# Values first, q and k of the forgetting attention and four dilated tiles as seven-product blocks, all through DRAM

## The chip, the core and the metric

One core of one Trainium2 chip runs the whole kernel in one launch. The metric is the device time of one execution in microseconds, lower is better, given as the median of several runs. TensorE multiplies matrices (PE in the views; PEld is its weight load), VectorE (DVE), ScalarE (ACT) and GpSimd (POOL) do elementwise work, and SyncE (SP) mostly starts transfers. Each engine works through its own queue in a fixed order, and waits at its head for what the next instruction needs.

## The reference

One decoder layer on x of 1024 tokens by 1024 channels, in float32:

```python
h = rms_norm(x, norm_mix_g)
proj = h @ w_in            # q, k, v of 3 dilated groups (256 wide each), then q, k, v of FoX (512 wide each), 8 forget logits, 2 x 1024 gates
...                        # dilated attention of each group; the groups are joined by their softmax denominators
...                        # FoX: softmax(q.k / 8 + sum of log f between key and query), 8 heads of 64, causal
gates = sigmoid(proj[..., o4:] + b_gate)
x = x + (gate0 * (dil @ w_dil_out) + gate1 * (fox @ w_fox_out)) @ w_out
...                        # then a SwiGLU feed-forward of width 2816 and a last norm
```

FoX is the forgetting attention: the logits get the cumulated log of a forget gate, c[t] - c[s].

## The kernel before

Every large product splits each operand in a high part (type fp32r) and a low part, the rest (`split`, L94 to L96: the high part by ScalarE, the low part by VectorE) and multiplying three times (`mm3`, L98 to L101): high by high, high by low, low by high. `projT` (L183) does the same for a transposed result with its lines L189, L190 and L193. One tile of 128 output channels for all 1024 tokens is therefore 2 halves x 8 slices of the depth x 3 = 48 products of 512 columns. A scheduler places all instructions ahead of the run: each engine gets one fixed order. Two sorts of PSUM banks exist: `pd` (the main program) and `pf` (filler).

The stages, in the order of the program:

- **x tiles and FoX values** (L271 to L316). For each of eight tiles of 128 tokens: norm, transpose into hT (L166, L171, split at L95/L96), then `values` of the tile before (L296): two groups of 24 products, 256 and 264 columns wide, where the last 8 columns are the forget logits (L307). The values stay in SBUF (`vf`).
- **Running sums** (L317 to L352, `cums`): log of the forget gate from the logits, in nine small operations on VectorE and ScalarE (L328 to L338), a product with a triangle and one with ones (L342, L343), and `negc` (L345 to L350).
- **FoX attention** (L354 to L468): four pairs of heads. `fox_proj` makes q and k of a pair (two tiles of 48 products), then come scores, maximum, exponentials, values and denominators for two halves of the queries. Scores of a unit stand ahead of the values of the unit before.
- **Dilated attention** (L474 to L650): tables for the distance bias, `dilv` (the values of the three groups, L509 to L521), then for two pairs of heads (u) and two halves of the queries (b) scores (L262), exponentials, values (L632), denominators (L635), `finish` (L243 to L253) and the store of the output (L638).
- **Merge** (L658 to L700): `load_o` reads the attention outputs back (L669) and splits them into `oh` and `ol`; `merge` multiplies each with its output weights (`projT`, L189 first), and with the gate.
- The output projection, then the feed-forward with its seven-product blocks (`up`, L853, 84 products instead of 96 for two tiles, from four combinations of its input and from three combinations of its weights made on GpSimd, L844 to L849), and the last norm.

Filler: `ahead` (L213) makes one tile of 48 products into the banks `pf`, evacuates it on ScalarE (L223) and stores it to DRAM (L224). There are 28: the 12 q and k tiles of the dilated attention (`dil_ahead`), and the 16 gate tiles (`gates_ahead`). They have their own weight buffers. The scheduler places their products wherever the main program's would wait; they run beside FoX, the dilated values, the dilated attention and the merge.

Of the kernel before, what the change touches and what calls it, by code (L numbers as in the profile page):

```python
# [15 lines left out]
P = 128  # L16
# [31 lines left out]
def layer_kernel(  # L48
# [152 lines left out]


    g_dram = dpool.tile([2 * KT, P, S], F32, name="g_dram")
    qk_dram = dpool.tile([2, 3, 2, P, S], F32, name="qk_dram")
    STR = ((1, 4, 8), (1, 8, 8))
    f_ctx = pool_of("ahead", 1, side="right")
    fpool = f_ctx.__enter__()
# [5 lines left out]
    def ahead(c0, dst, dl=1, sc=1.0):  # L213
        pf = [psf.tile([P, HALF], F32, tag="f", name=nm("pf")) for _ in range(2)]
        for c in range(2):
            w = load_w(w_in[c * HALF:(c + 1) * HALF, c0:c0 + P], 4, P, tag="fw", pool=fpool, rpool=fpool)
            for hh in range(2):
                for k in range(4):
                    mm3(pf[hh][:], w[:, k], hT[hh][:, 4 * c + k], c == 0 and k == 0, c == 1 and k == 3)
        n = HALF // dl  # L220
        st = fpool.tile([P, dl, S // dl], F32, tag="fst", name=nm("fst"), bufs=2)
# [4 lines left out]
    def dil_ahead():  # L226
        for u in range(2):
            for g in range(3):
                for a in range(2):
                    ahead(a * DIL_W + g * 256 + u * P, qk_dram[u, g, a], STR[a][g], SCALE if a == 0 else 1.0)  # L230

    def gates_ahead():
        for br, dt in merge_order:
            ahead(GATE0 + (br * KT + dt) * P, g_dram[br * KT + dt])
# [36 lines left out]
    with pool_of("fox", 1) as spool:  # L271
        lf = spool.tile([P, NT, 8], F32, name="lf", bufs=1)

        with pool_of("foxv", 2) as vpool:
            xts, last_x = [], [None]

            def load_x():
                i = len(xts)
                if i < NT:
                    xts.append(vpool.tile([P, D], F32, tag="xt", name=nm("xt"), bufs=4))  # L280
                    last_x[0] = nc.sync.dma_start(out=xts[i][:], in_=x[i * P:(i + 1) * P, :])

            load_x()
            gain1 = load_gain(vpool, norm_mix_g)
            nc.gpsimd.memset(ones[:], 1.0)
            vf = spool.tile([P, NT, 4, 2, DH], F32, name="vf", bufs=1)
            bg = cpool.tile([P, 16], F32, name="bg")
            bf = cpool.tile([P, 8], F32, name="bf")
            nc.gpsimd.dma_start(out=bf[0:1, :], in_=b_fgt[0:1, :])
            with nc.allow_non_contiguous_dma("per-partition gate bias"):  # L290
                nc.gpsimd.dma_start(out=bg[:], in_=b_gate[0].rearrange("(k p) -> p k", p=P))
            nc.gpsimd.partition_broadcast(bf[:], bf[0:1, :])
            wv = load_w(w_in[:, FOX0 + 2 * FOX_W:GATE0], KT, FOX_W + 8, tag="wv", bufs=1, pool=vpool,
                        chunk=P, rpool=vpool, rbufs=3, shared=2 * P, between=load_x)

            def values(i):  # L296
                hh, c = divmod(i * P, HALF)
                for c0, n in ((0, 256), (256, 264)):
                    pv = pd()
                    for k in range(KT):  # L300
                        mm3(pv[:, :n], hT[hh][:, k, c:c + P], wv[:, k, c0:c0 + n], k == 0, k == KT - 1)
                    p0 = c0 // 128
                    nc.vector.tensor_copy(
                        vf[:, i, p0:p0 + 2],
                        pv[:, :256].rearrange("p (a b d) -> p a b d", a=2, b=2))
                    if n == 264:
                        nc.vector.tensor_tensor(out=lf[:, i, :], in0=pv[:, 256:264], in1=bf[:],  # L307
# [661 lines left out]
```

## Time and profile before

| what | before |
|---|---|
| median of 3 runs | 1524.32 us (1521.35 to 1524.67) |
| profiled execution | 1523.66 us |
| its span, first to last instruction | 1522.0 us |
| PE / PEld busy | 1486.5 / 1213.7 us |
| DVE / ACT / POOL busy | 841.7 / 526.0 / 355.9 us |
| mean granted TensorE clock | 0.994 |
| moved by DMA | 148.56 MB |

The profiled execution is one run of the same program under the hardware profiler; the 1.7 us between it and its span lie before its first and after its last instruction. A row of a group reads: line, engine, operation, tile written <- tiles read, size, count, then busy time and mean ns of one, then the idle time of that engine just before and what ended it. A matmul's row gives the time from its start to its end; since matmuls overlap in the pipeline, what one costs is the distance from its start to the next one's start. A row of the timeline starts with its start time and its length.

### The profile page before, as it was taken

The page shows a single profiled execution, that of the slowest core. Times are in us where ns is not written, and L with a number is a line of the kernel's source. Part 1 is how long each engine was busy: PE and PEld are TensorE (multiplying, and loading weights), DVE is VectorE, ACT ScalarE, POOL GpSimd, SP SyncE. Part 2 cuts the span into 40 slices and gives each one's busy share as a digit, 9 for nine tenths or more (in the row PEclk, how much of TensorE's full clock was granted, in tenths as well). Part 3 has the DMA queues.
Part 4 walks back from the last instruction along what each step waited for, and adds up shares of the span by engine and source line. Part 5 has one row for each costly group of instructions (what it writes and reads, how often), then busy time and mean ns, then how long its engine had stood idle before and what let it go on. Part 6 is the DMA issues. An engine that isn't in the chain of part 4 may idle for free.

```text
span 1522.0 us, 18443 instructions
## 1 busy us (share of the span) xinstructions
PE 1486.5 (98%) x7172; PEld 1213.7 (80%) x7172; DVE 841.7 (55%) x1329; ACT 526.0 (35%) x828; POOL 355.9 (23%) x303
## 2 busy tenths in 40 slices
PE   6999999999999999999999999999999999999997
PEld 6987777777997778888888778888888887888886
DVE  6439687683129983115628854444444445856546
ACT  5246566553003244224315422222222225312113
POOL 0012224231001110000000245555555552140000
PEclk9999999999999999999999999999999999999999
DMA  8012211134113226334613122222222225642202
GB/s 251 14 57 62 66 60 43 35 91 132 70 35 132 70 77 218 104 100 149 239 56 138 42 69 84 83 84 83 83 84 84 83 98 198 205 136 86 95 14 97
DMA packets 130471, 148.56 MB, mean 98 GB/s; under 512 B 6352, under 2 KB 104656, under 8 KB 130384
## 3 DMA queue, kind: packets, MB, share of 16 engines
q1 hardware_dynamic: 117712, 103.86, 22.4%
q10 hardware_dynamic: 6768, 22.55, 4.1%
q0 software_dynamic: 5904, 20.98, 3.7%
q8 instruction: 56, 0.92, 0.2%
q14 instruction: 31, 0.25, 0.0%
HBM read 109.62 MB, written 37.75 MB: 97 GB/s over the span
## 4 chain that ended last, share of the span: by engine, by line
PE 89%; DMA 3%; ACT 2%; DVE 2%; POOL 2%; issue 1%; SPq 1%; ACTq 0%; DVEq 0%
PE pd L774 20%; PE pd L99 10%; PE pd L100 10%; PE pd L101 10%; PE pf L99 7%; PE pf L100 7%; PE pf L101 7%; PE pd L189 4%; PE pd L193 4%; PE pd L190 4%; PE pd L448 2%; DMA wr<-in_w_ffn_in_dram 2%; ACT wh L95 1%; PE pd L262 1%; PE pd L397 1%; PE pd L398 1%
## 5 line engine op out<-in xcount | busy, mean ns | idle before, releaser
L95 ACT ACTIVATE wh<-wr 128x1024 fp32r<-128x1024 f32 (+2 forms) x187 | 154.7, 836 | 472.6 <-PE pf L100 153.9
L96 DVE TENSOR_TENSOR wl<-wr,wh 128x1024 fp32r<-128x1024 f32 (+2 forms) x187 | 181.1, 974 | 205.0 <-ACT wh L95 198.4
L774 PE MATMUL pd<-hT_t,wh 128*128 128x512 f32 x640 | 198.4, 391 | 2.4 <-ACT c L860 2.4
L99 PE MATMUL pf<-hT_t,wh 128*128 128x512 f32 x448 | 177.0, 395 | 0.0
L100 PE MATMUL pf<-hT_t,wh 128*128 128x512 f32 x448 | 176.7, 394 | 0.0
L101 PE MATMUL pf<-hT_t,wl 128*128 128x512 f32 x448 | 174.1, 394 | 0.0
L774 PE MATMUL pd<-tT,wh 128*128 128x512 f32 x480 | 148.2, 390 | 0.4 <-DVE v L778 0.4
L774 PEld LDWEIGHTS pd<-hT_t,wh 128*128 128x128 f32 x640 | 120.6, 189 | 27.6 <-ACT c L860 2.8
L99 PE MATMUL pd<-wh,wh 128*128 128x512 f32 x352 | 138.0, 393 | 3.6 <-DVE acc L920 2.3
L100 PE MATMUL pd<-wl,wh 128*128 128x512 f32 x352 | 137.6, 391 | 0.0
L101 PE MATMUL pd<-wh,wl 128*128 128x512 f32 x352 | 137.6, 391 | 0.0
L99 PE MATMUL pd<-wh,hT_t 128*128 128x512 f32 (+2 forms) x384 | 128.1, 343 | 5.2 <-ACT wh L95 3.5
L100 PE MATMUL pd<-wl,hT_t 128*128 128x512 f32 (+2 forms) x384 | 131.3, 343 | 0.8 <-DVE t L155 0.6
L101 PE MATMUL pd<-wh,hT_t 128*128 128x512 f32 (+2 forms) x384 | 131.0, 342 | 0.0
L774 PE MATMUL pd<-hT_t,wl 128*128 128x512 f32 x320 | 126.6, 396 | 0.6 <-DVE wl L96 0.2
L920 DVE TENSOR_TENSOR acc<-pd,acc 128x512 f32<-128x512 f32 x128 | 86.0, 686 | 70.7 <-PE pd L101 70.5
L844 POOL TENSOR_TENSOR s<-wr 128x512 f32<-128x512 f32 x20 | 34.5, 1723 | 332.2 <-DVE tT L96 264.4
L774 PEld LDWEIGHTS pd<-tT,wh 128*128 128x128 f32 x480 | 90.3, 188 | 19.6 <-DVE v L778 0.8
L99 PEld LDWEIGHTS pf<-hT_t,wh 128*128 128x128 f32 x448 | 84.9, 190 | 20.7 <-issue 2.5
L101 PEld LDWEIGHTS pf<-hT_t,wl 128*128 128x128 f32 x448 | 84.6, 189 | 20.5 <-issue 3.1
L100 PEld LDWEIGHTS pf<-hT_t,wh 128*128 128x128 f32 x448 | 84.8, 189 | 19.8 <-issue 2.8
L774 PE MATMUL pd<-tT,wl 128*128 128x512 f32 x240 | 93.2, 389 | 0.0
(198 smaller groups left out, 2647.4 us busy)
## 6 DMA issues: line engine op xcount, KB each, us to landing
wr<-in_w_ffn_in_dram SPq DMA_DIRECT2D x44, 512.0 KB, 4.0
wr<-in_w_in_dram SPq DMA_DIRECT2D x56, 256.0 KB, 3.0
wr<-a_dram SPq DMA_DIRECT2D x22, 512.0 KB, 4.2
wr<-in_w_ffn_down_dram SPq DMA_DIRECT2D x22, 512.0 KB, 3.7
a_dram<-a POOLq DMA_DIRECT2D x20, 512.0 KB, 5.0
wr<-in_w_in_dram SPq DMA_DIRECT2D x18, 512.0 KB, 4.4
g_dram<-fst ACTq DMA_DIRECT2D x16, 512.0 KB, 3.2
land<-g_dram SPq DMA_DIRECT2D x16, 512.0 KB, 3.4
```

The lines of the kernel that those rows point to most:

```text
L95: nc.scalar.activation(out=hi, in_=src, func=AF.Copy)
L96: nc.vector.tensor_tensor(out=lo, in0=src, in1=hi.bitcast(F32), op=ALU.subtract)
L99: nc.tensor.matmul(psum, w.hi, m.hi, start=start, stop=False)
L100: nc.tensor.matmul(psum, w.hi, m.lo, start=False, stop=False)
L101: last_mm[0] = nc.tensor.matmul(psum, w.lo, m.hi, start=False, stop=stop)
L189: nc.tensor.matmul(pt[hh][:], w.hi[:, k], m.hi, start=(k == 0), stop=False)
L190: nc.tensor.matmul(pt[hh][:], w.hi[:, k], m.lo, start=False, stop=False)
L193: nc.tensor.matmul(pt[hh][:], w.lo[:, k], m.hi, start=False, stop=(k == kt - 1))
L448: nc.tensor.matmul(po[half[e], HALF - width[j]:], vf[:, j, pr, e], L[:, off[j]:off[j + 1]], start=(j == nj - 1), stop=(j == 0), skip_group ...
L774: last_mm[0] = nc.tensor.matmul(bank[:], p, q, start=first and k == 0 and n == 0, stop=k == 3 and n == 2, skip_group_check=True)
L844: nc.gpsimd.tensor_tensor(out=s12[:, :4], in0=u1, in1=u2, op=ALU.add)
L920: nc.vector.tensor_tensor(out=acc[:, t, cs], in0=pt[:], in1=acc[:, t, cs], op=ALU.add)
```

## The change

1. **FoX values** leave the attention's pool: they are computed as before, but for tiles 2 to 7 as one group of 24 products 512 columns wide, without the forget logits, and each tile is stored to DRAM (`vf_dram`, on GpSimd's queue). The attention loads all of them in one transfer.
2. **Dilated values** (`dilv`) come right after, ahead of both attentions: first group 0 with the forget logits beside it (`w0`, 264 columns), then groups 1 and 2 together (`w12`, 512 columns). ScalarE evacuates them (VectorE did) and they go to `vd_dram`.
3. **Combinations.** Beside that, `form` makes four combinations T1 to T4 of the quarters of h (16 adds of 128x1024 on VectorE, and their splits). They stay in SBUF until the projections end.
4. **The running sums** come after the dilated values, with `lf` and `negc` now in a pool of their own.
5. **Projections.** Six blocks make two tiles each with seven half-products instead of eight (84 products of 512 columns): four for q and k of FoX, two for q and k of the dilated groups 0 and 1 of u = 0. The weights' combinations are made on GpSimd (`left_side`). Results go to DRAM (`fqk_dram`, `dqk_dram`). All of this has no filler.
6. **Attentions.** `fox_qk` loads q and k of a pair from DRAM instead of computing them, and splits them. The filler that remains is 24 tiles: 8 dilated q and k tiles (`BESIDE`) and the 16 gates. `ahead` loads its weights as one tile through the common weight buffers. The dilated attention loads its values from DRAM.
7. The feed-forward's helpers (`raw_w`, `pair_of`, `prod`, `left_side`) move up to be shared; its work is the same. From the output projection on, TensorE's order is the same.

The core of the diff:

```diff
-    def ahead(c0, dst, dl=1, sc=1.0):
+    def ahead(pool, c0, dst, dl=1, sc=1.0):
...
-        for c in range(2):
-            w = load_w(w_in[c * HALF:(c + 1) * HALF, c0:c0 + P], 4, P, tag="fw", pool=fpool, rpool=fpool)
...
+        w = load_w(w_in[:, c0:c0 + P], KT, P)
+        for hh in range(2):
+            for k in range(KT):
+                mm3(pf[hh][:], w[:, k], hT[hh][:, k], k == 0, k == KT - 1)
...
+    TWOS = [[(0, g, a) for g in range(2)] for a in range(2)]
+    BESIDE = [(0, 2, 0), (0, 2, 1)] + [(1, g, a) for g in range(3) for a in range(2)]
...
+    def left_side(pool, rg, ru, bufs):
+        g1, g2, u1, u2 = rg[:, :4], rg[:, 4:], ru[:, :4], ru[:, 4:]
+        A1 = pair_of(rg[:])
+        s12 = pool.tile([P, KT, P], F32, tag="s", name=nm("s12"), bufs=2)
+        nc.gpsimd.tensor_tensor(out=s12[:, :4], in0=u1, in1=u2, op=ALU.add)
+        nc.gpsimd.tensor_tensor(out=s12[:, 4:], in0=s12[:, :4], in1=g1, op=ALU.subtract)
+        S12 = pair_of(s12[:], KT, pool, "s12", bufs)
...
+    def projections(pool, T, c, dst, dls, sc):
+        T1, T2, T3, T4 = T
+        A1, S12, S34, A22 = left_side(pool, *[raw_w(w_in[:, c0:c0 + P]) for c0 in c], 1)
...
+        prod(b1, A1[:, :4], B11, True)
+        copy(flat[0], b1)
+        prod(b2, S12[:, 4:], T2, True)
+        join(flat[1], b2, cc)
+        prod(b1, A1[:, 4:], B21)
+        copy(o1[:, :, :n1], b1, dls[0])
+        prod(b2, S34[:, :4], T3)
+        join(flat[2], b2, cc)
+        prod(b3, S12[:, :4], T1, True)
+        join(o2[:, :, n2:], b3, v3, dls[1])
+        prod(b2, A22, T4)
+        join(o2[:, :, :n2], b2, cc, dls[1])
+        prod(b3, S34[:, 4:], B22)
+        join(o1[:, :, n1:], b3, v2, dls[0])
...
         def values(i):
+            n = 256 if i < 2 else FOX_W
+            for c0 in range(0, FOX_W, n):
...
+                nc.vector.tensor_copy(st[:, c0:c0 + n], pv[:, :n])
+            nc.gpsimd.dma_start(out=vf_dram[i], in_=st[:])
...
+        def form(k0):
...
+            back(f3, B11)
+            back(f2, B12)
+            back(f4, B22)
+            vec(f1, f2, f3)
+            keep(T1, f1)
+            vec(f2, f4, f2)
+            keep(T3, f2)
+            vec(f4, f4, f1)
+            keep(T2, f4)
+            back(f3, B21)
+            vec(f3, f3, f4)
+            keep(T4, f3)
...
+            for g0, w, n in ((0, w0, 264), (1, w12, 512)):
+                for tt in range(NT):
...
+                    nc.scalar.activation(out=st[:, :m], in_=pv[:, :m], func=AF.Copy)
...
+            form(0)
+            form(2)
...
+        with pool_of("proj", 1) as upool:
+            for pr in range(0, 4, 2):
+                for a in range(2):
+                    c0 = FOX0 + a * FOX_W + pr * P
+                    projections(upool, T, (c0, c0 + P), [fqk_dram[a, pr + i] for i in range(2)], (1, 1), 1.0)
+            for two in TWOS:
+                projections(upool, T, [dil_cols(*t) for t in two], [dqk_dram[t] for t in two],
+                            [STR[a][g] for u, g, a in two], (SCALE, 1.0)[two[0][2]])
...
-        def fox_proj(pool, ql, pr):
+        def fox_qk(pool, ql, pr):
...
+                    raw = pool.tile([P, S], F32, tag="qraw", name=nm("qraw"), bufs=2)
+                    for at in half:
+                        nc.sync.dma_start(out=raw[at, :], in_=fqk_dram[a, pr, half[e], :])
+                    nc.scalar.activation(out=xs[e][:], in_=raw[:], func=AF.Copy, scale=sc)
...
-    with tc.issue_after(last_x[0].ins):
-        dil_ahead()
+    for u, g, a in BESIDE:
+        ahead(fpool, dil_cols(u, g, a), dqk_dram[u, g, a], STR[a][g], (SCALE, 1.0)[a])
...
-    with tc.issue_after(last_x[0].ins):
-        gates_ahead()
+    for br, dt in merge_order:
+        n = br * KT + dt
+        ahead(fpool, GATE0 + n * P, g_dram[n])
```

How the instructions move is shown at three places.

First, VectorE at the end of the FoX values. Before, the copies of the last tiles (`vf`) and the logits (`lf`) are followed by the running sums (L328 on):

```order
84 L303 COPY vf<-pd_700 128x256
85 L303 COPY vf<-pd_726 128x256
86 L307 TENSOR_TENSOR lf<-pd_726,bf 128x8
87 L303 COPY vf<-pd_753 128x256
88 L303 COPY vf<-pd_779 128x256
89 L307 TENSOR_TENSOR lf<-pd_779,bf 128x8
90 L328 TENSOR_SCALAR t_816<-lf 128x64
91 L329 TENSOR_TENSOR az<-lf,t_816 128x64
```

In the changed kernel adds of the combinations (L400, tiles f) stand there, then the copy of the last FoX values (L378), and behind it the low parts of w0, the weights of the dilated values of group 0 (L96 wv, three chunks), ahead of the combinations' splits (tT):

```order
74 L400 TENSOR_TENSOR f_1148<-f_1150,f_1148 128x1024
75 L400 TENSOR_TENSOR f_1149<-hT_t 128x1024
76 L400 TENSOR_TENSOR f_1150<-f_1150,f_1147 128x1024
77 L400 TENSOR_TENSOR f_1149<-f_1149,f_1150 128x1024
78 L378 COPY vst_623<-pd_624 128x512
79 L96 TENSOR_TENSOR wv_662<-wr_663,wv_661 128x8x128
80 L96 TENSOR_TENSOR wv_662<-wr_667,wv_661 128x8x128
81 L96 TENSOR_TENSOR wv_662<-wr_671,wv_661 128x8x8
82 L96 TENSOR_TENSOR tT_655<-f_1147,tT_655 128x1024
```

The low parts of these weights now stand behind a copy that needs the last value product, and no filler stands in the order there.

Second, TensorE around the two products of the running sums (`lf` with `upper` and with `ones`). Before, filler of a gate or a dilated tile (pf) stands ahead of them and a product of q behind them:

```order
435 L100 MATMUL pf_2555<-hT_t,wh_2587 128x512
436 L101 MATMUL pf_2555<-hT_t,wl_2588 128x512
437 L99 MATMUL pf_2556<-hT_t,wh_2587 128x512
438 L342 MATMUL pd_828<-lf,upper 128x64
439 L343 MATMUL pd_828<-lf,ones 128x64
440 L189 MATMUL pd_859<-hT_t,wh_853 128x512
441 L190 MATMUL pd_859<-hT_t,wh_853 128x512
```

In the changed kernel the last products of the dilated values (`wv` with `hT_t`) stand ahead, and the first block of the projections (L272) behind:

```order
638 L99 MATMUL pd_1119<-wv_659,hT_t 128x512
639 L100 MATMUL pd_1119<-wv_660,hT_t 128x512
640 L101 MATMUL pd_1119<-wv_659,hT_t 128x512
641 L475 MATMUL pd_1208<-lf,upper 128x64
642 L476 MATMUL pd_1208<-lf,ones 128x64
643 L272 MATMUL pd_1251<-hT_t,wh_1229 128x512 x2
644 L272 MATMUL pd_1251<-hT_t,wl_1230 128x512
645 L272 MATMUL pd_1251<-hT_t,wh_1229 128x512 x2
```

The sums' products moved from the middle of filler to the seam between the dilated values and the projections.

Third, TensorE at the end of the dilated attention: the last products with values (vd), the denominators (Mx with ones), filler (pf), and the merge's first products (oh). Before, 63 filler products stand between the denominators and the merge:

```order
2680 L632 MATMUL pd_4408<-L_541_4236,vd 64x64
2681 L632 MATMUL pd_4408<-L_540_4235,vd 64x64
2682 L635 MATMUL pd_4409<-Mx_4242,ones 64x512
2683 L635 MATMUL pd_4409<-Mx_4241,ones 64x512
2684 L100 MATMUL pf_4916<-hT_t,wh_4948 128x512
2685 L101 MATMUL pf_4916<-hT_t,wl_4949 128x512
...
2746 L101 MATMUL pf_4983<-hT_t,wl_5015 128x512
2747 L189 MATMUL pd_5542<-oh_5514,wh_5536 128x512
2748 L189 MATMUL pd_5543<-oh_5514,wh_5536 128x512
```

In the changed kernel four do:

```order
2695 L761 MATMUL pd_4350<-L_602_4177,vd 64x64
2696 L764 MATMUL pd_4351<-Mx_4184,ones 64x512
2697 L764 MATMUL pd_4351<-Mx_4183,ones 64x512
2698 L101 MATMUL pf_5297<-hT_t,wl_5299 128x512
2699 L99 MATMUL pf_5297<-hT_t,wh_5298 128x512
2700 L100 MATMUL pf_5297<-hT_t,wh_5298 128x512
2701 L101 MATMUL pf_5297<-hT_t,wl_5299 128x512
2702 L189 MATMUL pd_5388<-oh_5360,wh_5382 128x512
2703 L189 MATMUL pd_5389<-oh_5360,wh_5382 128x512
```

All gate tiles are now made ahead of this point; before, 399 filler products came after these denominators, most of them inside the merge.

247 lines of the change are left out of this document (127 added, 120 removed).

## The prediction

> **What bounds the kernel now.** I read the page first: the span, the busy times, the chain of waits by engine, and the costliest groups.
>
> ```profile
> span 1522.0 us, 18443 instructions
> PE 1486.5 (98%) x7172; PEld 1213.7 (80%) x7172; DVE 841.7 (55%) x1329; ACT 526.0 (35%) x828; POOL 355.9 (23%) x303
> PE 89%; DMA 3%; ACT 2%; DVE 2%; POOL 2%; issue 1%; SPq 1%; ACTq 0%; DVEq 0%
> L99 PE MATMUL pf<-hT_t,wh 128*128 128x512 f32 x448 | 177.0, 395 | 0.0
> ```
>
> TensorE is busy 1486.5 of 1522.0 us and makes up 89% of the chain, so a matmul that goes is worth its whole step, and 35 us at most lie in waits. The filler (the pf group, one of three lines with 448 each) never waited: it always stands ready when an attention does not. Next come TensorE's waits by what they waited for, and the timeline around the one in the changed part, the start of the dilated values:
>
> ```profile
> PE pt L171 <- DVE hn L166: 9.8, 1, 9.8
> PE pd L99 <- ACT wh L95: 3.5, 1, 3.5
> PE pd L262 <- DVE L L552: 1.6, 1, 1.6
> ...
> 360.68 1.07 PE L99 MATMUL pd<-wh,hT_t 128*128 128x256 f32 x6 [3.53 <-ACT wh L95]
> 361.55 0.63 PE L99 MATMUL pf<-hT_t,wh 128*128 128x512 f32 x1
> 361.98 0.63 PE L100 MATMUL pf<-hT_t,wh 128*128 128x512 f32 x1
> ...
> 364.90 0.40 PE L99 MATMUL pf<-hT_t,wh 128*128 128x512 f32 x1
> 365.14 0.39 PE L100 MATMUL pf<-hT_t,wh 128*128 128x512 f32 x1
> ```
>
> Two prices are read here. A 512-column step is 0.43 us right after the 3.53 us wait (361.55 to 361.98). The eight steps from 361.55 to 364.90 took 3.35 us; at 0.227 us each, the warm step read below, they would have taken 1.81. With 0.15 us on the six small products before them, a wait of this size costs itself **plus 1.7 us** of slow clock. The first wait, 9.8 us, is the start of the program and stays; the third, 1.6 us, stands at the first dilated scores.
>
> Last, a table by stretches, to see where the other engines come close: two pairs of the forgetting attention (62 us each), the first part of the dilated attention, the start of the merge, and a stretch of merge with no filler in it.
>
> ```profile
> 140.00:202.00 62.00, 62.00 (x296) 47.16 (x295) 43.53 (x77) 38.30 (x72) 15.24 (x21) 1.00 0.20 60
> 202.00:264.00 62.00, 62.00 (x295) 47.21 (x294) 48.49 (x87) 36.93 (x69) 18.24 (x22) 1.00 0.18 52
> 449.00:490.00 41.00, 39.41 (x280) 28.82 (x279) 38.15 (x66) 12.67 (x20) 6.39 (x3) 0.96 0.37 128
> 581.00:594.00 13.00, 13.00 (x59) 10.76 (x58) 4.92 (x7) 4.99 (x8) 2.69 (x5) 1.00 0.69 250
> 700.00:735.00 35.00, 35.00 (x156) 29.00 (x155) 27.16 (x47) 18.86 (x27) 0.00 (x0) 1.00 0.57 184
> ```
>
> The columns after the length are PE, PEld, DVE, ACT, POOL, then clock, DMA share and GB/s. TensorE is full in all but one; where VectorE reached 38.15 of 41 us, TensorE lost 1.59 us and the clock fell to 0.96.
>
> **Part 1: products saved.** Two steps are needed, of 264 and of 512 columns:
>
> ```profile
> 54.77 0.29 PE L99 MATMUL pd<-wh,hT_t 128*128 128x264 f32 x1
> 57.54 0.28 PE L101 MATMUL pd<-wh,hT_t 128*128 128x264 f32 x1
> ...
> 593.43 0.39 PE L99 MATMUL pf<-hT_t,wh 128*128 128x512 f32 x1
> 594.11 1.07 PE L189 MATMUL pd<-oh,wh 128*128 128x512 f32 x4
> ```
>
> From 54.77 to 57.54 are 23 steps, so 0.120 us each; from 593.43 to 594.11 are three, so 0.227. Six blocks take 84 products where two plain tiles took 96: 72 x 0.227 = **16.3 us**. Six of the eight value tiles become 24 products of 512 columns (5.44 us) instead of 48 of 256 or 264 (5.78): **2.0 us**. The forget logits move to the dilated values of group 0, whose products get 264 columns instead of 256: nothing. Sum −18.3. The 3.53 us wait and its 1.7 us of slow clock stand at a place that is gone: **−5.2**.
>
> The combinations of h, sixteen adds on VectorE and their splits, and the round trips of q, k and values through DRAM lie beside products; I price them where they come between two.
>
> **Part 2: values to dilated values, no filler any more.** The first six products on w0's high half can start at once; the next need its low half, and VectorE's queue has three low splits behind the copy of the last value tile, which waits for TensorE. VectorE's prices:
>
> ```profile
> L96 DVE TENSOR_TENSOR wl<-wr,wh 128x1024 fp32r<-128x1024 f32 x94 | 118.6, 1268 | 118.9 <-ACT wh L95 118.4
> L552 DVE SCALAR_TENSOR_TENSOR L<-R,pd 128x512 f32<-128x512 f32 x8 | 5.5, 692 | 3.2 <-PE pd L262 3.2
> ```
>
> A 128x512 operation out of PSUM is 0.69 us (the copy), a split 1.27; the third split has 64 elements a row, at most 0.2. After the last value product: 0.69 + 2 x 1.27 + 0.2 = 3.4, and some 0.5 for the result to reach VectorE, less 6 x 0.12 of products: 3.2 us idle, plus 1.7: **+4.9** (3 without the slow clock, 6.5 with a slower split).
>
> **Part 3: dilated values to projections.** The running sums of the forget logits were beside filler; now TensorE's queue has their two products ahead of the first block, and their buffers lie where the dilated values' weights lay, so they cannot start earlier. Their length before:
>
> ```profile
> 70.77 0.20 DVE L328 TENSOR_SCALAR t<-lf 128x64 f32<-128x64 f32 x1
> 73.43 0.23 DVE L338 SCALAR_TENSOR_TENSOR lf<-lf,az 128x64 f32<-128x64 f32 x1
> ...
> 78.47 0.33 PE L342 MATMUL pd<-lf,upper 128*128 128x64 f32 x2
> 80.52 0.22 DVE L350 SCALAR_TENSOR_TENSOR negc<-pd,tot 128x56 f32<-128x56 f32 x1
> ```
>
> From L328 to L338's end is 2.9 us, and its Exp stands on ScalarE behind the last evacuation of the dilated values: about 3.3 us idle. Then 24 products of A1 can run: 24 x 0.227 + 1.7 of slow clock, so TensorE is out of work 3.3 + 0.4 + 7.1 = 10.8 us after the last value product. Meanwhile the sums end 2.3 us after their products start (78.47 to 80.74), at 5.6, and only then may GpSimd write the weights' combination S12, whose buffer lies on theirs. GpSimd and the splits cost:
>
> ```profile
> L844 POOL TENSOR_TENSOR s<-wr 128x512 f32<-128x512 f32 x20 | 34.5, 1723 | 332.2 <-DVE tT L96 264.4
> L848 POOL TENSOR_TENSOR s<-wr,wr 128x512 f32<-128x512 f32 x20 | 26.5, 1327 | 0.0
> L845 POOL TENSOR_TENSOR s<-s,wr 128x512 f32<-128x512 f32 x20 | 26.2, 1312 | 1.4
> L95 ACT ACTIVATE wh<-s 128x1024 fp32r<-128x1024 f32 x40 | 42.4, 1060 | 103.7 <-POOL s L845 82.5 <-PE pd L774 21.2
> ```
>
> 5.6 + 1.72 + 1.33 + 1.31 = 10.0, ScalarE's high half 11.0, VectorE's low half 12.3. So about 1 us more of waiting: 3.3 + 1.7 + 1.0 = **+6.0** (4 to 8). The later blocks have 84 x 0.227 = 19 us each for some 5.7 us of GpSimd: TensorE sets their pace.
>
> **Part 4: into and through the forgetting attention.** The nearest rows for a 512 KB transfer:
>
> ```profile
> g_dram<-fst ACTq DMA_DIRECT2D x16, 512.0 KB, 3.2
> land<-g_dram SPq DMA_DIRECT2D x16, 512.0 KB, 3.4
> ```
>
> q and k now come from DRAM through two buffers that are free only when the last block has read the combinations. About 14 us of products (62 x 0.227) stand before the first score that needs k; two rounds of load (3.4), high half (1.06) and low half (1.27) are 11.5 us, and a load of all values runs beside them: **+1** (0 to 4). In the attention itself TensorE's work per pair falls from 62 to some 50 us (568 filler products, 128.8 us, and about 74 us of attention by the widths of its products, over four pairs), and VectorE keeps about 44 of its 43.5 to 48.5 us: nine tenths. The row at 449 is the nearest, 0.93, where the loss was 1.59 us and about 1 of slow clock in 41. **+2.5** for all four (0 to 8, three such losses). In the dilated attention the filler between its first scores and last values is 343 products, before 331: 0 (−2.6, if the wait of 1.6 us and its slow clock go, to +2).
>
> **Part 5: start of the merge.** Before, what ran there:
>
> ```profile
> 578.70 1.03 PE L635 MATMUL pd<-Mx,ones 128*64 128x512 f32 x4
> 583.51 0.55 POOL L638 DMA_DIRECT2D o_dram<-o  x1 [21.32 <-DVE o L253]
> 584.13 2.18 POOL L669 DMA_DIRECT2D land<-o_dram  x4
> 591.12 1.06 ACT L95 ACTIVATE oh<-land 128x1024 fp32r<-128x1024 f32 x1 [1.39 <-DMA land<-o_dram]
> ```
>
> The denominators end at 579.73; the loads stand on GpSimd's queue behind the store of the last output, 4.4 us later; the first load is split at 592.18. These 12.4 us were hidden by 63 filler products (63 x 0.227 = 14.3). In the new order four are left, 0.9 us: all gates are spent inside the attentions. TensorE waits 11.4 us, plus 1.7: **+13.1**. What could shorten it is the load, 7.0 us here (584.13 to 591.12) with the DMA engines 0.69 busy. With the 3.4 us of the gates' loads the wait is 7.8, so 9.5 in all; with the next chunks 3 us late, 16. I take the row of the same load. Past it the merge runs without filler at full rate, as the stretch at 700 shows, so the filler that left the merge is only moved.
>
> **A rule against the trace.** Right after the 3.53 us wait the step was 0.43 us. The Trainium skill ("TensorE: Matmul & The Clock Gate", on the HAM clock gate) says that the clock is halved after an idle window of about 3.4 us and comes back after as long a busy one. By that rule the waits of 3.2 and 3.3 us need not cost the slow clock, and the sum would be 3.4 us lower. The trace does not agree that a shorter wait is safe: the stretch with only the 1.6 us wait shows a clock of 0.96.
>
> **Sum.** −18.3 −5.2 + 4.9 + 6.0 + 1.0 + 2.5 + 13.1 = +4.0 on the profiled execution's 1523.66; that stands 0.66 below the median of the runs, 1524.32, so **1528.3 us**. A measurement of this kernel cannot tell 0.2% (3 us) from no change: slower is above 1527.4, faster below 1521.3.
>
> **Rivals.**
> 1. *The two handovers are covered, and it comes out faster.* If the low splits of w0 are done before the last value copy, and S12 before A1's products end, parts 2 and 3 cost nothing: 1528.3 − 10.9 = **1517.4**. It decides from 7 us of the two. For it: the forming has slack, and both engines are half idle in the page. Against it: the order of VectorE's queue. Chance 0.23.
> 2. *VectorE becomes the bound of the forgetting attention.* Part 4 at its upper end and beyond: with VectorE's work at 48.5 us a pair instead of 44, a pair has no slack and each hand from ScalarE or GpSimd shows; three losses of 2.6 more, +8: **1536**. For it: the row at 449. Against it: 62 us pairs at 0.78 lost nothing. Chance 0.18.
> 3. *The merge's first load is quick* (the filler's loads and stores no longer run beside it): 3.6 us less, **1524.7**, no change. Chance 0.14.
> 4. My sum as it stands, 1528.3, with the lesser terms inside their ends: 0.45.
>
> **Numbers.** Faster: rival 1 (0.23) and a tail of my sum (0.05). Same: rival 3 (0.14) and the part of my sum under 1527.4 (0.14). Slower: the rest. Range: 1515.0 (rival 1 with two low ends) to 1538.5 (rival 2 with one more upper end); my own case alone spans 1523 to 1534.
>
> **What would show it.** In the changed profile: TensorE waits of about 3 us before the low-half products of the first dilated values and before the sums' product; the first S12 product late by 1 us; a wait of 8 to 12 us ahead of L189, put down to ScalarE's oh; 0.43 us steps after each; pairs of the forgetting attention of 50 us with VectorE near nine tenths; a block of 84 products in 19 us. I am wrong if the merge starts without a wait, if the blocks run at more than 20 us, or if the handovers show no wait.

## The result: 1.3% slower, and the profile after

The changed kernel takes 1543.63 us (median of 4, 1542.41 to 1547.0) against 1524.34 before: a ratio of 1.0134 (95% interval 1.0114 to 1.0155). The forecast was 1528.3 with a range up to 1538.5: the sign was right, the size was not. The profiled execution took 1544.29 us, 20.6 more than that of before.

The page of the changed kernel, first its span, its busy times and its chain:

```profile
span 1542.5 us, 18138 instructions
PE 1478.9 (96%) x6956; PEld 1196.4 (78%) x6956; DVE 895.5 (58%) x1321; ACT 536.0 (35%) x808; POOL 419.1 (27%) x351
PE 79%; DMA 6%; DVE 4%; POOL 4%; ACT 3%; issue 2%; SPq 1%; ACTq 0%; POOLq 0%; DVEq 0%
```

TensorE is 7.6 us less busy, but it now idles 63.6 us (1542.5 − 1478.9) instead of 35.5, and its share of the chain fell from 89 to 79%. Its waits, by what they waited for:

```profile
PE pd L189 <- ACT oh L95: 11.3, 1, 11.3
PE pt L171 <- DVE hn L166: 9.8, 1, 9.8
PE pf L99 <- ACT fst L224: 7.8, 2, 6.4
PE pd L475 <- DVE lf L471: 3.6, 1, 3.6
...
PE pd L338 <- DMA dqk<-dqk_dram: 2.7, 2, 2.0
...
PE pd L100 <- DVE wv L96: 2.0, 1, 2.0
```

The first, fourth and last are the three seams of the forecast: merge, running sums, low halves of w0. The third is new: filler itself waits. The timeline there, at the start of the forgetting attention:

```profile
270.36 25.22 SPq L513 DMA_DIRECT2D qraw<-fqk_dram  x12
...
270.62 0.93 POOL L503 DMA_DIRECT2D vf<-vf_dram  x1 [13.69 <-PE pd L272]
...
281.25 1.06 ACT L514 ACTIVATE qx<-qraw 128x1024 fp32r<-128x1024 f32 x1 [6.30 <-DMA qraw<-fqk_dram]
...
290.47 1.06 ACT L514 ACTIVATE kx<-qraw 128x1024 fp32r<-128x1024 f32 x1 [4.27 <-DMA qraw<-fqk_dram]
291.43 0.58 ACT L224 ACTIVATE fst<-pf 128x512 f32<-128x512 f32 x1
292.06 0.79 PE L99 MATMUL pf<-hT_t,wh 128*128 128x512 f32 x1 [6.38 <-ACT fst L224]
292.65 0.63 PE L100 MATMUL pf<-hT_t,wh 128*128 128x512 f32 x1
293.08 0.63 PE L538 MATMUL pd<-qx,kx 128*128 128x512 f32 x1
```

The q and k loads and the 2 MB load of all values start within 0.3 us of each other. The first q is there after 10.9 us (270.36 to 281.25), its buffer is free for the first k only after that, and k comes at 290.47. The DMA view from 262 to 295, in forty slices of 0.8 us (the busy share of the DMA engines in tenths, and the rate), and transfers of that stretch (KB each, us to landing):

```profile
DMA  0028920000199999999999999999999589710046
GB/s 0 0 21 230 335 70 0 0 0 0 30 223 343 318 214 179 243 253 313 258 318 318 338 432 417 407 412 422 412 417 377 238 263 243 214 35 0 0 45 228
...
qraw<-fqk_dram SPq DMA_DIRECT2D x12, 256.0 KB, 5.4
vf<-vf_dram POOLq DMA_DIRECT2D x1, 2048.0 KB, 15.6
...
dqk_dram<-qo POOLq DMA_DIRECT2D x2, 512.0 KB, 15.5
```

From 271 on the DMA engines are busy at nine tenths or more, 0.98 on the mean from 270.4 to 281.2, so whatever moves beside the first q can take time from it: the load of all values, and two stores of the last block's results. That they do is what e2 tests. The rate was not at its highest then (179 to 343 GB/s); from 281 to 287, when the first q is there, the core moves 407 to 432 GB/s. The Trainium skill ("DMA: Bandwidth & Descriptors", Specifications) puts the ceiling of the fabric at 435 GB/s; the trace agrees, as no slice of this stretch passes it.

The start of the merge went as forecast, a wait of 11.3 us and slow steps behind it:

```profile
671.01 1.03 PE L764 MATMUL pd<-Mx,ones 128*64 128x512 f32 x4
...
676.70 0.55 POOL L767 DMA_DIRECT2D o_dram<-o  x1 [21.58 <-DVE o L329]
677.37 1.12 POOL L799 DMA_DIRECT2D land<-o_dram  x2
...
684.50 2.07 PE L189 MATMUL pd<-oh,wh 128*128 128x512 f32 x4 [11.31 <-ACT oh L95]
```

To set the stages against each other (e2 and e12 are experiments, below) I take five marks from the timelines, each the start of the product or group named, and the filler products between them, each worth 0.227 us:

| mark, us | before | after | e2 | e12 |
|---|---|---|---|---|
| first forgetting score | 105.9 | 293.1 | 287.6 | 287.6 |
| last forgetting denominator | 343.3 | 504.9 | 493.2 | 493.1 |
| last dilated denominator | 578.7 | 671.0 | 655.4 | 647.3 |
| first product of the output projection | 735.5 | 752.7 | 736.0 | 731.2 |
| last product | 1513.0 | 1533.1 | 1513.5 | 1508.9 |
| filler ahead of the first score | 60 | 98 | 105 | 105 |
| in the forgetting attention | 425 | 568 | 550 | 550 |
| to the end of the dilated attention | 460 | 482 | 454 | 420 |
| between it and the merge | 63 | 4 | 43 | 77 |
| inside the merge | 336 | 0 | 0 | 0 |

So the forgetting attention without filler took 211.8 − 568 x 0.227 = 82.9 us; before, less its 425 filler products and the 288 of q and k of three pairs, 75.5.

### The profile page after: what moved, and what is told of

It reads as the page before. It is cut to its first block, busy times and chain, and to the rows that moved or that the text cites. A ratio compares the mean times of both kernels' runs of the same rounds, so it can differ in the third digit from the quotient of the medians.

```text
span 1542.5 us, 18138 instructions
## 1 busy us (share of the span) xinstructions
PE 1478.9 (96%) x6956; PEld 1196.4 (78%) x6956; DVE 895.5 (58%) x1321; ACT 536.0 (35%) x808; POOL 419.1 (27%) x351
## 4 chain that ended last, share of the span: by engine, by line
PE 79%; DMA 6%; DVE 4%; POOL 4%; ACT 3%; issue 2%; SPq 1%; ACTq 0%; POOLq 0%; DVEq 0%
PE pd L272 25%; PE pd L100 10%; PE pd L101 10%; PE pd L99 10%; PE pf L101 4%; PE pf L100 4%; PE pf L99 4%; DMA wr<-in_w_ffn_in_dram 2%; ACT wh L95 2%; PE pd L189 2%; PE pd L190 2%; PE pd L193 2%; PE pd L589 2%; POOL sg L969 1%; DVE wl L96 1%
## 5 line engine op out<-in xcount | busy, mean ns | idle before, releaser
L96 DVE TENSOR_TENSOR wl<-wr,wh 128x1024 fp32r<-128x1024 f32 (+2 forms) x152 | 166.9, 1102 | 143.7 <-ACT wh L95 143.4
L272 PE MATMUL pd<-hT_t,wh 128*128 128x512 f32 x784 | 244.7, 393 | 3.0 <-ACT c L952 2.3
L272 PE MATMUL pd<-tT,wh 128*128 128x512 f32 x672 | 206.4, 389 | 0.9 <-DVE v L884 0.6
L272 PEld LDWEIGHTS pd<-hT_t,wh 128*128 128x128 f32 x784 | 148.3, 190 | 34.5 <-ACT c L952 2.7
L99 PE MATMUL pf<-hT_t,wh 128*128 128x512 f32 x384 | 151.7, 395 | 8.0 <-ACT fst L224 7.8
L272 PE MATMUL pd<-hT_t,wl 128*128 128x512 f32 x392 | 155.0, 396 | 1.5 <-DVE wl L96 1.1
L100 PE MATMUL pf<-hT_t,wh 128*128 128x512 f32 x384 | 151.9, 396 | 0.0
L272 PEld LDWEIGHTS pd<-tT,wh 128*128 128x128 f32 x672 | 126.0, 188 | 27.9 <-DVE v L884 1.1
L272 PE MATMUL pd<-tT,wl 128*128 128x512 f32 x336 | 129.7, 389 | 0.2 <-DVE wl L96 0.2
L96 DVE TENSOR_TENSOR wl<-s,wh 128x1024 fp32r<-128x1024 f32 x52 | 64.8, 1246 | 67.8 <-ACT wh L95 67.8
L95 ACT ACTIVATE wh<-s 128x1024 fp32r<-128x1024 f32 x52 | 55.1, 1060 | 131.4 <-POOL s L260 98.4
L272 PEld LDWEIGHTS pd<-hT_t,wl 128*128 128x128 f32 x392 | 74.4, 190 | 22.4 <-DVE wl L96 7.1
```

Of the source, the lines that this page charges most:

```text
L95: nc.scalar.activation(out=hi, in_=src, func=AF.Copy)
L96: nc.vector.tensor_tensor(out=lo, in0=src, in1=hi.bitcast(F32), op=ALU.subtract)
L99: nc.tensor.matmul(psum, w.hi, m.hi, start=start, stop=False)
L100: nc.tensor.matmul(psum, w.hi, m.lo, start=False, stop=False)
L272: last_mm[0] = nc.tensor.matmul(bank[:], p, q, start=first and k == 0 and n == 0, stop=k == 3 and n == 2, skip_group_check=True)
```

## The experiments

My theory was that the loss beyond the forecast is the collision of loads at the start of the forgetting attention, and filler spent where nothing waited. The rivals: VectorE bounds the attention, or engine queues hold the filler. Times of single runs stand beside one of the kernel before of 1522.96 us (e1 to e4), or beside a median of 1524.09 (e5 to e8) or 1523.42 (e9 to e12). The changed kernel was not run again beside them, and its own four runs lie 4.6 us apart, so differences of a few us are read from the marks and waits of each profile, not from the time. An edit also moves filler, since each kernel gets its order anew; so each run is read with its filler taken off.

**e1, the sums' tiles elsewhere.**

```diff
-        with pool_of("cums", 1) as cums:
+            cw = wpool.tile([P, KT, P], F32, tag="wr", name=nm("cw"), bufs=2)
```

> Changed kernel, with the running sums' small tiles put in a common weight buffer instead of where the dilated values' weights lay, so that the sums can run beside the products of groups 1 and 2; nothing is left out. Theory A (the seam between dilated values and projections costs its waits and slow clock, and nothing gives it back): the 3.6 us wait ahead of the sums' product and the small ones behind it are gone, the time falls by 5 to 7 us against the changed kernel, to about 1537. Rival B (whatever is saved before the forgetting attention is lost again, since that attention is set by VectorE or by its loads): the wait goes, and the time falls by less than 2 us.

Measured: 1534.96 us, 8.7 less than the changed kernel, but not by what was meant. The wait on the sums went, and another came a few products later, from the profile of e1:

```profile
151.09 2.07 PE L272 MATMUL pd<-tT,wh 128*128 128x512 f32 x4 [4.48 <-ACT wh L95]
```

The borrowed buffer was one that the block's own weights needed; the first score came at 294.3, not earlier. The gain is behind it: the order left 24 filler products for the merge instead of 4, and the wait there was 5.9 us. By the marks, with the filler taken off, 5.4 us were won there and 3.5 in the forgetting attention. Theory A named the seam, and the seam gave nothing; that the time came near its 1537 was luck, by filler that an edit here moved 500 us later.

**e2, the values' load behind the first q and k.**

```diff
-        nc.gpsimd.dma_start(out=vf[:]..., in_=vf_dram...)
...
                 qk = fox_qk(apool, ql, pr)
+                if pr == 0:
+                    with tc.issue_after(last_raw[0].ins):
+                        nc.sync.dma_start(out=vf[:]..., in_=vf_dram...)
```

> Changed kernel, with the 2 MB load of all forgetting values issued behind the first pair's q and k loads on one queue instead of beside them; nothing is left out. Theory A (the start of the forgetting attention waits for the first q and k, which are late because the value load takes their bandwidth): the first load lands some 5 us earlier, TensorE's wait of 6.4 us at 292 shrinks to under 2 us, and the time falls by 5 to 8 us, to about 1536 to 1538. Rival B (the chain of two buffers, two rounds of load, split and release, sets it, not the bandwidth): the wait shrinks by at most 2 us. Rival C: the values come late instead, and a wait of the same size appears at the first products with them.

Measured: 1523.86 us, 20 less. Its timeline at the same place:

```profile
270.38 12.32 SPq L514 DMA_DIRECT2D qraw<-fqk_dram  x8
...
276.21 1.06 ACT L515 ACTIVATE qx<-qraw 128x1024 fp32r<-128x1024 f32 x1 [1.24 <-DMA qraw<-fqk_dram]
...
282.95 0.38 SPq L607 DMA_DIRECT2D vf<-vf_dram  x1
283.84 1.06 ACT L515 ACTIVATE kx<-qraw 128x1024 fp32r<-128x1024 f32 x1 [2.91 <-DMA qraw<-fqk_dram]
...
287.61 0.39 PE L539 MATMUL pd<-qx,kx 128*128 128x512 f32 x1
```

The first q is split 5.0 us earlier, k 6.6, the 6.4 us wait is gone, and no values come late: A holds on the wait, B and C fall. Its 5 to 8 us for the whole time were too few. By the marks, with the filler taken off, 7.1 us are won ahead of the first score (5.5 us and 7 more products), 2.2 in the attention, and 10.0 between the last dilated denominator and the output projection, where 43 filler products are left instead of 4; the dilated attention gives 2.4 back, and the last 2.9 come behind the merge, from work that is the same. More was won at the merge than at the wait that was removed.

**e3, high halves of the first pair on VectorE.**

```diff
-                    nc.scalar.activation(out=xs[e][:], in_=raw[:], func=AF.Copy, scale=sc)
+                    if pr == 0:
+                        nc.vector.tensor_scalar(out=xs[e][:], in0=raw[:], scalar1=sc, scalar2=None, op0=ALU.mult)
```

> Changed kernel, with the high halves of the first pair's q and k made on VectorE instead of ScalarE; nothing is left out. The profile puts TensorE's 6.4 us wait at 292 down to ScalarE's evacuation of filler, which stands behind those high halves. Theory A (the scores' q and k are late; the filler's wait is only the first one seen): the wait moves to the scores' products or stays about as long in sum, 5 to 8 us, and the time changes by less than 3 us. Rival B (ScalarE's queue order is what holds the filler, and freeing it lets TensorE go on): the wait goes to under 2 us and the time falls by 5 to 8 us.

Measured: the wait did what A says, it moved to the scores, in the profile of e3:

```profile
291.91 0.79 PE L541 MATMUL pd<-qx,kx 128*128 128x512 f32 x1 [6.80 <-DVE kx L524]
```

So ScalarE's queue was only where it was seen first; the k was late. But the time fell to 1529.09, 14.5 less, which A did not expect. By the order, 42 filler products were left for the merge, whose wait was 2.6 us. The part of A that said "less than 3 us" was wrong because it took the filler's places as fixed.

**e4, the merge's loads on SyncE's queue.**

```diff
-                nc.gpsimd.dma_start(out=raw[:], in_=o_dram[c0 + c])
+                nc.sync.dma_start(out=raw[:], in_=o_dram[c0 + c])
```

> Changed kernel, with the merge's loads of the attention outputs issued on SyncE's queue instead of GpSimd's, where they stood behind the store of the last dilated output; nothing is left out. The forgetting outputs that the first products need have been in DRAM for long. Theory A (the wait of 11.3 us at the start of the merge is this queue order, with its load): the loads are issued during the last dilated unit, the wait falls to 1 to 3 us, and the time falls by 9 to 13 us, to about 1531 to 1535. Rival B (the wait is set by the buffers of the dilated attention, which come free only with its last output): the wait falls by at most 2 us.

Measured: 1540.14 us, 3.5 less, between the two. The same filler as in the changed kernel, the wait 8.0 instead of 11.3 us. In the profile of e4 (the DMA queue's row says how long the queue was held):

```profile
633.37 42.52 SPq L118 DMA_DIRECT2D wr<-in_w_fox_out_dram  x4
...
676.05 2.35 SPq L799 DMA_DIRECT2D land<-o_dram  x4
...
682.33 2.07 PE L189 MATMUL pd<-oh,wh 128*128 128x512 f32 x4 [7.99 <-ACT oh L95]
```

The loads now stand behind four weight loads that wait for the merge's weight buffers: one queue's wait was exchanged for another's.

**e6, one half-product of each block twice**, on the kernel of e2.

```diff
         prod(b3, S34[:, 4:], B22)
+        prod(b3, S34[:, 4:], B22)
```

> The kernel of the second experiment with one half-product of each block run twice (12 products of 512 columns more in each of six blocks, 72 in all; the added copy makes the first tile of each block wrong). In the order of this kernel only 4 filler products are left between the last denominators and the merge, in the second experiment's 43. Theory A (blocks are bound by TensorE, and filler left for the merge is worth its full length): 72 x 0.227 = 16.3 us more for the blocks and 39 x 0.227 = 8.9 us more at the merge, together about 1549. Rival B (blocks have slack, since GpSimd and the splits set their pace): the blocks lengthen by under 8 us. Rival C (the start of the merge does not depend on the filler left): 16.3 us more alone, about 1540.

Measured: 1550.59 us. The first score came at 302.9 instead of 287.6, with 5 filler products fewer ahead of it: 15.24 + 1.14 = 16.4 us for 72 products, 0.227 each. The blocks are bound by TensorE, and their saving is what the forecast put. The merge, with 4 products left, waited 10.9 us where e2 waited 1.9. A holds in both halves.

**e7, one gate tile held back for the merge.**

```diff
-    for br, dt in merge_order:
+    for br, dt in merge_order[:-1]:
...
+    with tc.issue_after(last_den[0].ins):
+        for br, dt in merge_order[-1:]:
```

> Changed kernel with the last gate tile held back: its 48 products may stand only behind the last denominators, so that 48 instead of 4 cover the start of the merge, and the dilated attention has 299 instead of 343; nothing is left out. Theory A (the dilated attention has filler to spare, 44 products there hide nothing): the merge's wait of 11.3 us falls to 1 to 2 us, the dilated attention gets shorter by the products it lost, and the time falls by 9 to 12 us, to about 1533. Rival B (the attention needs that filler): the dilated attention keeps its length with new waits of about 10 us in it, and the time stays within 3 us of the changed kernel.

Measured: 1542.0 us, 1.6 less than the changed kernel's median and within 0.5 of its lowest run, so no change. Its profile:

```profile
662.96 6.65 PE L763 MATMUL pd<-L,vd 128*64 128x256 f32 x64 [5.66 <-ACT L L737]
...
683.01 1.20 PE L189 MATMUL pd<-oh,wh 128*128 128x512 f32 x4 [1.44 <-ACT oh L95]
```

The merge's wait went, and a wait of 5.7 us came before the last unit's values, which those products had covered. The dilated attention, with 44 products fewer (10.0 us), got 2.2 us shorter. B is the nearer: filler is a stock of 24 tiles, and taken from the dilated attention it is missed there.

**e8 and e12, the dilated values' load behind the first dilated q and k**, on the kernel of e2.

```diff
-            nc.gpsimd.dma_start(out=vd[:, g]..., in_=vd_dram[g]...)
...
                 qk = dil_qk(apool, u)
+                if u == 0:
+                    with tc.issue_after(last_qk[0].ins):
+                        for g in range(3):
+                            nc.sync.dma_start(out=vd[:, g]..., in_=vd_dram[g]...)
```

> The kernel of the second experiment with the 3 MB load of the dilated values issued behind the first dilated q and k; nothing is left out. In the second experiment TensorE waited 1.9 and 4.1 us for those q and k. Theory A (the same collision of loads as at the forgetting attention): both waits go to under 1 us in sum, and with 77 instead of 43 filler products left for the merge its 1.9 us wait goes too: the time falls by 5 to 8 us, to about 1517. Rival B (the loads wait for their buffers, not for bandwidth): the waits stay.

> The kernel of the eighth experiment again, for its time with an interval: Theory A: 1514 to 1519, a ratio to the kernel before of 0.993 to 0.997. Rival B: the single time was luck of a run, and the ratio is within 0.998 to 1.002.

Measured: 1516.86 us in e8, and 1518.88 (median of 7) in e12, where the ratio to the kernel before is 0.9969 (0.9956 to 0.9982): this version beats both, the kernel before by 0.3%. Not for the reason of A, though. Both waits stayed, in the profile of e8:

```profile
507.81 0.46 DVE L640 SCALAR_TENSOR_TENSOR R<-oddf,R 128x128 f32<-128x128 f32 x1 [0.55 <-POOL R L633]
508.34 2.80 SPq L661 DMA_DIRECT2D dqk<-dqk_dram  x6
...
513.12 2.03 PE L338 MATMUL pd<-dqk,dqk 64*128 64x128 f32 x32 [1.23 <-DMA dqk<-dqk_dram]
520.89 1.44 PE L338 MATMUL pd<-dqk,dqk 64*128 64x128 f32 x10 [4.61 <-DMA dqk<-dqk_dram]
```

The q and k loads start right after the tables are built, whose scratch memory they reuse: B is right about the buffers. What was won is that 34 more filler products (77 instead of 43) stand at the merge, which no longer waits.

**e5, five edits together**: e1, e2, e8, the last value tile copied on ScalarE, and the merge's first loads on ScalarE's queue.

```diff
+                if i == NT - 1:
+                    nc.scalar.activation(out=st[:, c0:c0 + n], in_=pv[:, :n], func=AF.Copy)
...
+                (nc.scalar if br == 1 else nc.gpsimd).dma_start(out=raw[:], in_=o_dram[c0 + c])
```

> Changed kernel with five edits of order and place, nothing left out: the sums' tiles in a weight buffer (as in the first experiment), the values' load behind the first q and k (as in the second), the last value tile copied on ScalarE, the dilated values' load behind the first dilated q and k on one queue, and the merge's first loads issued on ScalarE's queue. Theory A (the loss against the forecast is made of waits at stage seams, each with its own cause, and filler spent where nothing waited): the seams go, 77 filler products are left for the start of the merge, and the time is 1508 to 1514, 10 to 16 us under the kernel before. Rival B (VectorE bounds the forgetting attention at nine tenths, and what seams give up turns up there): not under 1518.

Measured: 1523.5 us (median of 10), ratio 0.9995 (0.9983 to 1.0006): no change, and 4.6 more than e12, which has two of the five. The first score came at 290.4 instead of 287.6, with e1's wait for the weights (4.5 us) again in the seam. Copying the last value tile on ScalarE changed one wait for another: 2.7 us for the high halves of w0, behind that copy on ScalarE, instead of 2.0 for the low halves. 77 products at the merge made the last edit idle. Neither A nor B: the attention was as long as in e2 (205.6 us with 550 products), the seams did not go.

**e9, the sums behind the first block**, on the kernel of e8.

```diff
+                    if pr == a == 0:
+                        sums()
```

> The kernel of the eighth experiment with the running sums written behind the first block of the projections instead of ahead of it, their tiles in a pool of their own below the projections' pool; nothing is left out. The first experiment moved the sums' tiles, but into a weight buffer that the block's own weights need, and a wait of 4.5 us for those weights came in place of 3.6. Theory A (the seam is the sums standing between the last dilated value and the first block, in TensorE's queue and in memory): the wait of 3.6 us and its slow clock go, the small waits behind stay under 1.5 us, and the first score comes 4 to 6 us earlier than in the eighth experiment, at 282 to 284. Rival B (the block's own weights, loaded, combined and split after the last dilated value, set the seam): a wait of 3 to 5 us stays under another name and the first score comes less than 2 us earlier.

Measured: 1520.47 us (median of 7, ratio 0.9976, 0.9964 to 0.9988), first score at 289.3, later than in e8. The seam did close, as A says: 3.6 us went, 0.7 and 1.4 us were left, and the blocks were done 4.5 us earlier (the first q load starts at 265.87 instead of 270.42). Then, in the profile of e9:

```profile
274.26 1.09 ACT L224 ACTIVATE fst<-pf 128x512 f32<-128x512 f32 x2 [10.22 <-DMA dqk_dram<-qo]
...
274.91 0.80 PE L99 MATMUL pf<-hT_t,wh 128*128 128x512 f32 x1 [6.35 <-ACT fst L224]
```

Filler's first evacuation waits for the store of the last block's results, which was still on its way. I read this as one piece of memory used by both; another place for it was not tried.

**e10, more work on VectorE in the forgetting attention**, on the kernel of e8.

```diff
+                    if pr > 0:
+                        nc.vector.tensor_copy(raw[:], raw[:])
```

> The kernel of the eighth experiment with 12 more operations of 128x1024 on VectorE, one for each loaded q or k half of pairs 2 to 4, written back onto the buffer that is done with (no result changes). They are some 1.2 us each, 14 us in all, while VectorE has 174 of 193 us of work there. Measure: the time from the first score to the last denominator, less 0.227 us for each filler product in it, which is 80.6 us in the eighth experiment. Theory A (VectorE bounds the forgetting attention at nine tenths): it grows by 10 us or more. Rival B (VectorE has room, TensorE bounds): it grows by less than 4 us.

Measured: 1535.97 us. The two rows of the table by stretches, from the first score to the last denominator, e12 (the same kernel as e8) and then e10:

```profile
287.60:493.10 205.50, 203.27 (x965) 149.13 (x965) 177.62 (x302) 129.64 (x238) 86.06 (x87) 0.99 0.37 108
```

```profile
289.60:510.60 221.00, 216.21 (x1020) 159.04 (x1021) 183.80 (x315) 133.25 (x241) 83.74 (x87) 0.99 0.36 106
```

The copies took 0.69 us each, 8.1 in all, and VectorE's busy time rose by 6.2, not 14, so this asks less than was meant. Without filler the stage grew from 80.6 to 83.7 us, less than 4, which is B's number and not A's; but 3 of the 8 us show, so VectorE is not free either. The copies also hold the two load buffers longer, which was not set apart. The stage itself grew by 15.5 us, because the schedule put 605 filler products in it instead of 550, and 17 instead of 77 were left for the merge, which waited 7.8 us.

**e11, low halves of k on GpSimd**, on the kernel of e9.

```diff
-                        nc.vector.tensor_tensor(out=xs[e][rows, :], in0=raw[rows, :], in1=hi, op=ALU.subtract)
+                        (nc.gpsimd if pr else nc.vector).tensor_tensor(out=xs[e][rows, :], in0=raw[rows, :], in1=hi, op=ALU.subtract)
```

> The kernel of the ninth experiment with the low halves of k for pairs 2 to 4 made on GpSimd instead of VectorE, six operations of 1.2 us; nothing is left out. Same measure as in the tenth. Theory A (VectorE bounds): the attention less its filler gets 3 to 6 us shorter than in the ninth experiment. Rival B (it does not): within 2 us, and the total time within 3 us, apart from what the filler's new places change at the merge.

Measured: 1554.31 us, 33.8 more than e9. From its profile:

```profile
L527 POOL TENSOR_TENSOR kx<-qraw,kx 64x1024 fp32r<-64x1024 f32 x6 | 15.6, 2605 | 39.1 <-ACT kx L520 9.1 <-ACT rc L323 7.9 <-issue 7.7
...
347.69 0.80 PE L544 MATMUL pd<-qx,kx 128*128 128x512 f32 x1 [10.03 <-POOL kx L527]
```

The scores waited 21.8 us in all for k, which GpSimd came to late. It says nothing on whether VectorE bounds the stage; that stays open.

## Why the prediction was wrong, step by step

The forecast was +4.0 us on the profiled execution, and +20.6 was measured. Term by term, from the waits and the marks:

| term | forecast | measured |
|---|---|---|
| products saved, old wait gone | −23.5 | −23.5 (taken over; e6: 0.227 us each) |
| values to dilated values | +4.9 | +2.7 |
| dilated values to blocks | +6.0 | +6.5 |
| into the forgetting attention | +1.0 | +10.7 |
| in it | +2.5 | +5.2 |
| dilated attention | 0 | +1.5 |
| start of the merge | +13.1 | +14.6 |
| output projection and after | 0 | +2.9 |
| sum | +4.0 | +20.6 |

- **The step that failed is part 4**, "two rounds of load ... and a load of all values runs beside them: +1 (0 to 4)"; it is the one term that went far past its own ends. It took 3.4 us for a load from rows where little else ran, named the 2 MB load beside it, and gave it no price. The first q took 10.9 us; TensorE waited 6.4, and the slow steps up to 298 us cost 2.8 more (0.6 of it ahead of the first score): 9.2. e2 took the load away from there and won 7.1 + 2.2 = 9.3 up to the end of that attention, so this load is the cause. The other 1.5 us of the row are a wait of the first filler behind the blocks, for ScalarE's evacuation, which itself waits for VectorE's last result of the block; e2 has it too, so it is not the load, and the sum had no term for it.
- **In the attention** I priced three small stalls at 2.5; 82.9 us less the 2.2 of slow steps counted above, less the 75.5 of before, is 5.2. VectorE is busy 178.9 of 211.8 us there, 0.84, not nine tenths; that it is the reason is not shown, and the cause of these 5.2 stays open.
- **The first dilated q and k** (2.0 and 0.7 us of waits) had no term: loads that came from DRAM before too, but now into memory that comes free late (e8 took the 3 MB load beside them away, and the waits stayed). From the last forgetting to the last dilated denominator, without filler, 56.7 us, 1.0 of it the forgetting denominators themselves; before, 54.2 from the first dilated score on: 1.5 more, inside the ends given (−2.6 to +2).
- **The merge** was right in place, mechanism and price: four products, a load behind a store, 11.3 us. The size (14.6 from the last denominator to the output projection) is 1.5 more.
- **The seams** were right in mechanism. The first is 2.7 us (seven steps in 3.58 us where 0.84 was due): it left no slow clock, and no run shows the half microsecond put in for the result to reach VectorE (the last product's row ends at 66.86, the copy starts at 66.90). The second is 4.7 us of waits and 1.8 of slow clock. Its sum of 6.5 came out near the forecast partly by luck: the sums cost 3.6, but S12 only 0.4 where about 1 was put, and 0.7 is a wait for the evacuation of the block's first bank, which had no term.
- **The slow clock.** 2.02 us of idle time were followed by steps of 0.12 us, the full rate, and 3.63 us by steps of 0.43; but in the profile of before 1.56 us (up to 463.63) were enough for steps of 0.43. The Trainium skill ("TensorE: Matmul & The Clock Gate", HAM clock gate) halves the clock after an idle window of about 3.4 us; the first two agree with it, the third does not.
- **The tail** has the same TensorE order in all these kernels and took 775.5 to 780.4 us from its first product to its last: 2.9 is inside that scatter, and I would give it no cause.
- What the sum had no place for: **filler is a stock.** I took it as work that stands ready and costs its length wherever it runs. It does; but 24 tiles instead of 28, without the 8 tiles of q and k between scores, have to cover both attentions and the merge, and the order decides who goes without. e1, e3 and e10 moved 20 to 60 products between the attentions and the merge by an edit elsewhere, and with them 5 to 11 us at the merge. Its wait follows the products left for it: 11.3 us with 4 (10.9 in e6), 7.8 with 17 (e10), 5.9 with 24 (e1), 2.6 with 42 (e3), 1.9 with 43 (e2), 1.4 with 48 (e7, e9), none with 77 (e12). Only e4, which changed the loads' queue, is off this line: 8.0 with 4.

Of the rivals, the second (VectorE bounds, 1536) came nearest in time and is not shown as a cause; the first and third did not happen.

## What to carry to other kernels

When results go through DRAM, price each stage's first load with everything that starts at the same moment: put the tile that is needed first ahead of the bulk on one queue. Count filler as a stock with named customers before giving any of it up, and count it again in the order after every edit, since a schedule made ahead may spend it elsewhere. A wait removed in one queue or one piece of memory (e1, e4, e9) often stands in the next one; look at who reuses the memory before looking at speed.

## What the runs showed of the hardware

A subtraction of 64x1024 took 2.6 us on GpSimd (e11) and 1.2 on VectorE (L521 of the changed kernel, 1218 ns). A copy of 128x1024 within SBUF on VectorE took 0.69 us (12 of them in e10), where I had put 1.2 as for a two-operand operation. In the stretch from 262 to 295 of the changed kernel, in slices of 0.8 us, the core's transfers did not get past 432 GB/s. The load of the first q, 512 KB, took 10.9 us beside one of 2 MB started with it, and 5.8 with that one behind it (270.38 to 276.21 in e2).
